# A decoder trunk on one core: on which tiles of an expert block the pieces of gather and scatter are given, and behind which block gathering begins

## The chip, the core and the metric

One core of one Trainium2 chip runs the whole program. The metric is the device time of one execution in microseconds (us), lower is better. TensorE (PE; its weight loads are shown as PEld), VectorE (DVE), ScalarE (ACT), GpSimd (POOL) and SyncE (SP, which issues the loads of weights here) run their own instruction streams and wait for each other through semaphores.

## What is computed

Two layers of a decoder trunk for 256 tokens of width 1024, all in float32. Each layer has four token mixers, an output projection, a feed-forward part and a gated embedding. The feed-forward part of the second layer, the only place that the change touches, sends each token to the best two of eight experts:

```python
def swiglu(x, w_gate, w_up, w_down):
    return (jax.nn.silu(x @ w_gate) * (x @ w_up)) @ w_down

def moe_swiglu(x, router, w_gate, w_up, w_down):
    logits = (x @ router).astype(jnp.float32)
    top_val, top_idx = lax.top_k(logits, TOP_K)
    top_w = jax.nn.softmax(top_val, axis=-1)
    combine = jnp.sum(jax.nn.one_hot(top_idx, N_EXPERTS, ...) * top_w[..., None], axis=-2)
    out = jnp.zeros_like(x)
    for e in range(N_EXPERTS):
        out = out + combine[..., e:e + 1] * swiglu(x, w_gate[e], w_up[e], w_down[e])
    return out
```

An expert's hidden width is 3584.

## The kernel before, in words

**Places.** The eight experts are worked off in eight places, four large ones, L 0 to L 3 (up to 128 tokens, as the stationary side of 128 columns), and four small ones, S 0 to S 3 (up to 64 tokens; high and low halves of the tokens lie side by side in 128 columns). L 0 is the first expert; which experts go to the other places is found at run time by their numbers of tokens. A large and a small place run together, the small one a block behind.

**Blocks and tiles.** Each place has seven blocks of 512 hidden columns (NB = 7), and each block six weight tiles of 1 MB (128 x 2048 floats): t = 0 and 1 are gate tiles, 2 and 3 up tiles, 4 and 5 down tiles. The list STEPS fixes the order of all tiles. In the middle of the stage a block has twelve: L t0, S t0, L t1, then the two turns, S t1, L t2, S t2, L t3, S t3, and then the down tiles of the block before: L t4, S t4, L t5, S t5. An L tile is 12 matmuls of 512 columns (L283 to L285), an S tile 8 (L1344, L1345).

**A weight tile's way.** SP loads it into one of seven buffers `raw` (L212). Products are made of split numbers: ACT copies `raw` to `hi`, DVE subtracts to get `lo` (both in `split`; ACT and DVE instructions of the stage all show as L146, the wrapper that keeps each of the two engines in program order). There are five buffers `hi` and `lo`; `ahead(5, 1)` ahead of each tile keeps the splits of the coming tiles issued, so they stand in the queues of ACT and DVE ahead of whatever follows the tile. PE is kept in program order too (`in_order`).

**Turns.** Between L t1 and S t1 the hidden values of the block before are turned (`turn`): for L four transposes into a PSUM tile `e` (L300) and a split by ACT and DVE; for S sixteen matmuls of 64 columns into another tile `e` (L288), a SiLU on ACT, and then two closures: `times` (a DVE product that reads the same tile `e`) and `parts` (a split into `hs`). There are two PSUM banks for tiles `e`.

**Pieces.** `gather` fetches the tokens of the next two places: six DVE instructions make 0/1 selectors in `s` from `posx`, and then the list `later` gets a pause, four pieces (each 8 matmuls of 192 columns into a tile `e`, L288, then a split of the L columns into `x` by ACT and DVE and one of the S columns into `xs` by ACT and DVE) and two `turned_slots` (two transposes into a tile `e`, L300, an ACT copy). `scatter` splits a finished place's sums at once and puts two pauses and four pieces in `later`: each 2 matmuls of 512 columns into a tile `e` (L288) and one DVE instruction that adds to `h`. The main loop calls `some(1)` after every tile, which takes one entry off `later`. `turn` puts `times` and `parts` at its front, so that they come behind S t1 and L t2. Gathering for the places n + 1 begins behind the second down tile of block 4 of place L n.

So before the change, pieces come behind L t0, S t0, L t1, (turns, `times`, `parts`,) S t2, L t3 and so on, until the list is empty. An L place's scatter is called behind L t5 of the block after its last one, an S place's a block later behind S t5.

Of the kernel before, what the change touches and what calls it, by code (L numbers as in the profile page):

```python
# [84 lines left out]
def decoder_trunk(ctx: ExitStack, tc: tile.TileContext, A, out):  # L85
# [27 lines left out]
    def T(tag, shape, dt=F32, keep=False):  # L113
        count[0] += 1
        name = f"{tag}_{count[0]}"
        if phase and tag + "+" in phase["bufs"] and not keep:
            n = BUFS[tag] + phase["bufs"][tag + "+"]
            turn[tag] = (turn.get(tag, -1) + 1) % n
            if turn[tag] >= BUFS[tag]:
                return phase["pool"].tile(shape, dt, name=name, tag=tag + "+", bufs=n - BUFS[tag])  # L120
        if tag in BUFS and (keep or not (phase and tag in phase["bufs"])):
            return sb.tile(shape, dt, name=name, tag=tag, bufs=BUFS[tag])
        return phase["pool"].tile(shape, dt, name=name, tag=tag, bufs=phase["bufs"][tag])

    def PS(tag, shape, dt=F32):
        count[0] += 1
        return ps.tile(shape, dt, name=f"p{tag}_{count[0]}", tag="p" + tag, bufs=BUFS[tag])
# [96 lines left out]
    def split(x, o_hi, o_lo, note=True):  # L224
        a = act_copy(o_hi, x)
        b = V.tensor_tensor(o_lo, x, f(o_hi), op=ALU.subtract)  # L226
        if note:
            latest.update(act=a, dve=b)
        return a, b
# [4 lines left out]
    def ahead(n, parts=2, keep=False):  # L234

        while len(ready) < n:
            ready.append(new_split(parts, keep))
# [15 lines left out]
    @contextmanager  # L253
    def in_order():

        line.append(None)
        yield
        line.clear()
# [28 lines left out]
    def mm(o, l, r, start=True, stop=True):  # L287
        pe(PE.matmul(o, l, r, start=start, stop=stop, skip_group_check=True))  # L288
# [10 lines left out]
    def transpose(o, i):  # L299
        pe(PE.transpose(o, i, ident[:i.shape[0], :i.shape[0]]))  # L300
# [715 lines left out]
    def feed_forward(i, g_ffn, acc, rest):  # L1016
# [38 lines left out]
        if i == 0:  # L1055
            acc = ffn(xh, xl)
        else:
            acc = None
            moe(cn, xh, xl)
            embed = embedding()  # L1060
            for t in range(2):
                embed(t)
# [104 lines left out]
    def moe(cn, xh, xl):  # L1167
# [153 lines left out]
                if (kind, n) != ("L", 0):  # L1321
                    later.append(partial(turned_slots, kind, n, s, at_[kind]))

        later = []

        def pause():
            pass
# [19 lines left out]
        def gate_up(u, t):  # L1347

            gx = xg[u[:2]]
            g, q = divmod(t, 2)  # L1350
            if q == 0:
                out_[u] = PS("c", [P, 512])
            o = out_[u]
            wh, wl = [v.rearrange("p (k n) -> p k n", k=4) for v in pop_split(1)]
            for kk in range(4):
                k = 4 * q + kk
                lhs = (gx[:, 0, k, :], gx[:, 1, k, :]) if u[0] == "L" else gx[:, k, :]
                products(u, o, lhs, wh[:, kk, :], wl[:, kk, :], k == 0, k == NK - 1)
            if q == 0:
                return  # L1360
            if u[0] == "S":
                s = T("S2", [P, 512])
                act_copy(s, o)
                hid.setdefault(u, []).append(s)
            elif g == 0:
                s = T("S2", [P, 512])
                S.activation(s, o, AF.Silu)
                hid[u] = s
            else:
                V.tensor_tensor(hid[u], hid[u], o, op=ALU.mult)  # L1370

        def turn(u):

            s = hid.pop(u)
            if u[0] == "L":
                pt = PS("e", [P, 4, P])
                for c in range(4):
                    transpose(pt[:, c, :], s[:, c * P:(c + 1) * P])
                hh, hl = T("S2", [P, 4, P], F32R), T("S2", [P, 4, P], F32R)
                split(pt, hh, hl)  # L1380
                hT[u] = hh, hl
                return
            pt = PS("e", [P, 2, 4, 64])
            for g in range(2):
                for c in range(4):
                    mm(pt[:, g, c, :], s[g][:, c * P:(c + 1) * P], cf[:, CF["halves"]])
            a = T("S1", [P, 4, 64])
            S.activation(a, pt[:, 0], AF.Silu)

            def times():  # L1390
                V.tensor_tensor(a, a, pt[:, 1], op=ALU.mult)

            def parts():
                hs = T("S2", [P, 4, P], F32R)
                split(a, hs[:, :, :64], hs[:, :, 64:])
                hT[u] = hs

            later[:0] = [times, parts]

        def down(u, q):  # L1400
            p, b = u[:2], u[2]
            if b == 0 and q == 0:
                acc[p] = [PS("d" if u[0] == "L" else "c", [P, 512]) for _ in range(2)]
            wh, wl = [v.rearrange("p (k n) -> p k n", k=2) for v in pop_split(1)]
            for n in range(2):
                for kk in range(2):
                    c = 2 * q + kk
                    lhs = [v[:, c, :] for v in hT[u]] if u[0] == "L" else hT[u][:, c, :]
                    products(u, acc[p][n], lhs, wh[:, kk, n * 512:(n + 1) * 512],
                             wl[:, kk, n * 512:(n + 1) * 512], b == 0 and c == 0, b == NB - 1 and c == 3)  # L1410
            if q:
                del hT[u]
                if b == NB - 1:
                    scatter(p)
# [18 lines left out]
        def some(n=None):  # L1433
            while later and n != 0:
                later.pop(0)()
                n = n and n - 1
# [15 lines left out]
        with in_order():  # L1452
            for u, t in STEPS:
                if t is None:
                    for v in u:
                        turn(v)
                    done = dict(latest)
                    continue
                ahead(5, 1)
                if t < 4:  # L1460
                    gate_up(u, t)
                else:
                    down(u, t - 4)
                some(1)
                if t == 5 and u[0] == "L" and u[2] == 4 and u[1] < 3:
                    gather(("L", u[1] + 1), ("S", u[1] + 1))
        V.keep(False)
        S.keep(False)
# [227 lines left out]
```

## Time and profile before

| | |
|---|---|
| Time, median of 3 runs | 1669.14 us (1667.97 to 1673.68) |
| Profiled execution | 1667.4 us, of which the span 1665.4 us |
| PE, DVE, ACT busy, share of the span | 95%, 78%, 65% |
| Mean granted clock of PE | 0.973 |
| Expert stage, from its first to its last products | 690 to 1607 us of the span |
| Weights loaded in it | 336 tiles of 1 MB |

Times in rows are counted from the span's start. [...] "Idle before" is the time for which an engine sat idle ahead of an instruction, and behind the arrow stands what ended it. An instruction is shown in a group by the tiles it writes and reads (`pe`, `pc`, `pd` are PSUM tiles of the tags e, c, d).

### The profile page before, as it was taken

To read this page: it belongs to the slowest core of one execution; us is meant where nothing else is said; L and a number is where in the kernel's file an instruction comes from. 1 tells how busy PE (TensorE), PEld (TensorE's weight loads), DVE (VectorE), ACT (ScalarE), POOL (GpSimd) and SP (SyncE) were. 2 spreads that over 40 slices of the span, in tenths; PEclk is the share of its full clock that TensorE was granted. 3 is DMA by queue.
4 is the path that set the end of the run, shared out by engine and by line. 5 is a ranking of instruction groups with operands and counts; after the bars stand their busy time and mean duration, and the time that the engine had idled before them with its cause. 6 is when DMAs were issued, how large, how long until landed. Compare 5 with 4: busy or idle time off the path is not lost.

```text
span 1665.4 us, 22588 instructions
## 1 busy us (share of the span) xinstructions
PE 1580.6 (95%) x8523; PEld 1347.7 (81%) x8523; DVE 1299.9 (78%) x1464; ACT 1085.9 (65%) x1309; POOL 80.4 (5%) x116
## 2 busy tenths in 40 slices
PE   7998999999999989799989999989999989999998
PEld 7896799999888977688878778878778877788886
DVE  5578655445575786799979889979889979799995
ACT  5555554444455563688868668858768867688883
POOL 1024000000000141000000000000000000000000
PEclk9999999999999999899999999999999999899999
DMA  8431464545444222499999889979989979899980
GB/s 323 161 118 58 159 233 159 213 160 204 144 163 184 98 98 77 166 421 421 421 378 377 347 332 413 415 310 388 350 338 416 419 284 416 343 349 415 420 361 26
DMA packets 65488, 461.25 MB, mean 277 GB/s; under 512 B 7392, under 2 KB 7776, under 8 KB 12128
## 3 DMA queue, kind: packets, MB, share of 16 engines
q1 hardware_dynamic: 64224, 455.02, 69.4%
q10 hardware_dynamic: 1152, 4.76, 0.9%
q8 instruction: 68, 1.11, 0.3%
q14 instruction: 44, 0.36, 0.1%
HBM read 458.70 MB, written 1.05 MB: 276 GB/s over the span
## 4 chain that ended last, share of the span: by engine, by line
PE 38%; DVE 11%; issue 6%; ACT 2%; DMA 1%; POOLq 0%; POOL 0%; DVEq 0%; ACTq 0%
DVE lo L146 8%; PE pc L1344 7%; PE pc L1345 6%; PE pc L283 5%; PE pc L285 4%; PE pc L284 4%; PE pe L288 4%; ACT hi L146 2%; PE pd L283 2%; PE pd L284 2%; PE pd L285 2%; DMA raw<-in_moe_gu_dram 1%; DVE S L146 1%; DVE h L146 1%; PE pe L300 1%
## 5 line engine op out<-in xcount | busy, mean ns | idle before, releaser
L146 DVE TENSOR_TENSOR lo<-raw,hi 128x2048 fp32r<-128x2048 f32 x338 | 757.9, 2284 | 94.6 <-ACT hi L146 94.2
L146 ACT ACTIVATE hi<-raw 128x2048 fp32r<-128x2048 f32 x338 | 637.2, 1911 | 79.1 <-PE pd L285 23.1
L226 DVE TENSOR_TENSOR lo<-raw,hi 128x1024 fp32r<-128x1024 f32 (+3 forms) x188 | 201.2, 1113 | 122.7 <-ACT hi L160 122.4
L160 ACT ACTIVATE hi<-raw 128x1024 fp32r<-128x1024 f32 (+3 forms) x188 | 170.0, 966 | 120.4 <-PE pc L285 84.3
L283 PE MATMUL pc<-hi,x 128*128 128x512 f32 x512 | 203.6, 398 | 3.1 <-DVE order L1263 2.4
L285 PE MATMUL pc<-hi,x 128*128 128x512 f32 x512 | 202.0, 394 | 0.0
L284 PE MATMUL pc<-lo,x 128*128 128x512 f32 x512 | 202.0, 394 | 0.0
L1344 PE MATMUL pc<-hi,xs 128*128 128x512 f32 x448 | 186.5, 416 | 0.0
L283 PE MATMUL pd<-x,hi 128*128 128x256 f32 x640 | 182.4, 285 | 0.1
L1345 PE MATMUL pc<-lo,xs 128*128 128x512 f32 x448 | 182.4, 407 | 0.0
L285 PE MATMUL pd<-x,lo 128*128 128x256 f32 x640 | 182.1, 285 | 0.0
L284 PE MATMUL pd<-x,hi 128*128 128x256 f32 x640 | 181.5, 284 | 0.3 <-DVE x L226 0.3
L283 PEld LDWEIGHTS pd<-x,hi 128*128 128x128 f32 x640 | 122.4, 191 | 1.6 <-ACT x L160 0.3
L285 PEld LDWEIGHTS pd<-x,lo 128*128 128x128 f32 x640 | 122.3, 191 | 1.5 <-DVE lo L226 0.2
L284 PEld LDWEIGHTS pd<-x,hi 128*128 128x128 f32 x640 | 122.3, 191 | 1.2 <-DVE x L226 0.5
L283 PEld LDWEIGHTS pc<-hi,x 128*128 128x128 f32 x512 | 96.9, 189 | 25.5 <-issue 2.6
L285 PEld LDWEIGHTS pc<-hi,x 128*128 128x128 f32 x512 | 96.5, 188 | 22.8 <-DVE x L226 0.4
L284 PEld LDWEIGHTS pc<-lo,x 128*128 128x128 f32 x512 | 96.5, 188 | 22.1
L1344 PEld LDWEIGHTS pc<-hi,xs 128*128 128x128 f32 x448 | 88.9, 198 | 19.1
L1345 PEld LDWEIGHTS pc<-lo,xs 128*128 128x128 f32 x448 | 88.6, 198 | 19.3
L288 PE MATMUL pe<-cf,S 128*128 128x64 f32 (+1 forms) x452 | 66.4, 310 | 26.1 <-DVE h L146 13.2
L283 PE MATMUL pd<-hi,S 128*128 128x512 f32 x224 | 88.7, 396 | 0.0
(288 smaller groups left out, 2510.0 us busy)
## 6 DMA issues: line engine op xcount, KB each, us to landing
raw<-in_moe_gu_dram SPq DMA_DIRECT2D x224, 1024.0 KB, 7.1
raw<-in_moe_dn_dram SPq DMA_DIRECT2D x112, 1024.0 KB, 7.8
raw<-in_ffn_gu_dram SPq DMA_DIRECT2D x28, 1024.0 KB, 5.1
raw<-in_ffn_dn_dram SPq DMA_DIRECT2D x14, 1024.0 KB, 5.0
raw<-in_win_t_dram SPq DMA_DIRECT2D x16, 848.0 KB, 4.7
raw<-in_win_c_dram SPq DMA_DIRECT2D x12, 1024.0 KB, 6.6
raw<-in_cmp_w_dram SPq DMA_DIRECT2D x8, 1024.0 KB, 5.6
raw<-in_w_out_dram SPq DMA_DIRECT2D x8, 1024.0 KB, 4.9
```

Source lines behind the costliest of these rows:

```text
L146: ins = op(*args, **kw)
L160: return S.activation(o, i, AF.Copy, scale=scale)
L226: b = V.tensor_tensor(o_lo, x, f(o_hi), op=ALU.subtract)
L283: pe(PE.matmul(o, lh, rh, start=start, stop=False))
L284: pe(PE.matmul(o, lh, rl, start=False, stop=False))
L285: pe(PE.matmul(o, ll, rh, start=False, stop=stop))
L288: pe(PE.matmul(o, l, r, start=start, stop=stop, skip_group_check=True))
L300: pe(PE.transpose(o, i, ident[:i.shape[0], :i.shape[0]]))
L1344: pe(PE.matmul(o, lhs, rh, start=start, stop=False))
L1345: pe(PE.matmul(o, lhs, rl, start=False, stop=stop))
```

## The change

There are now two lists. `times` and `parts` go to a list `soon`. Behind each tile the loop takes an entry of `soon` if there is one; if there is none, it takes one of `later`, but only behind tiles with t of 2 to 5 (and behind every tile of the very first block). And `gather` is called behind block 3 of a place L n instead of block 4.

```diff
-        later = []
+
+        soon, later = [], []
...
-            later[:0] = [times, parts]
+            soon.extend([times, parts])
...
-                some(1)
-                if t == 5 and u[0] == "L" and u[2] == 4 and u[1] < 3:
+                if soon:
+                    soon.pop(0)()
+                elif t > 1 or u == ("L", 0, 0):
+                    some(1)
+                if t == 5 and u[0] == "L" and u[2] == 3 and u[1] < 3:
                     gather(("L", u[1] + 1), ("S", u[1] + 1))
```

## Rows read from the trace of the kernel before

**Rows 1.** The page's first part, the line of PE: busy us (share of the span), instructions.
```profile
PE 1580.6 (95%) x8523; PEld 1347.7 (81%) x8523; DVE 1299.9 (78%) x1464; ACT 1085.9 (65%) x1309; POOL 80.4 (5%) x116
```

**Rows 2.** Busy time by stretches, each from the start of one S turn to that of the next. Columns: stretch, its length, busy us and instructions of PE, PEld, DVE, ACT, POOL, then granted clock, busy share of the DMA engines, GB/s.
```profile
764.39:794.37 29.98, 29.98 (x143) 24.71 (x142) 28.82 (x17) 25.35 (x18) 0.00 (x0) 1.00 1.01 421
...
824.28:864.61 40.33, 34.35 (x167) 28.51 (x165) 35.72 (x30) 29.63 (x27) 0.00 (x0) 0.98 1.01 421
864.61:899.13 34.52, 34.52 (x152) 28.83 (x153) 27.03 (x18) 25.24 (x22) 0.00 (x0) 0.92 0.83 315
899.13:934.30 35.17, 31.80 (x148) 25.68 (x146) 33.86 (x24) 27.04 (x22) 0.00 (x0) 1.00 1.01 423
934.30:972.12 37.82, 35.08 (x147) 28.43 (x147) 31.74 (x22) 26.09 (x20) 0.00 (x0) 0.91 0.86 327
972.12:1006.33 34.21, 34.21 (x145) 28.26 (x146) 28.07 (x18) 24.36 (x17) 0.00 (x0) 0.90 0.85 318
1006.33:1036.36 30.03, 30.03 (x143) 24.70 (x141) 28.21 (x17) 25.00 (x19) 0.00 (x0) 1.00 1.01 420
```

**Rows 3.** Groups of instructions by line and shape in the stretch 690 to 1610 us, the two groups of PE matmuls with idle time ahead of them (the S turns; the L turns with the slots' transposes). Behind the first bar busy us and mean ns of one, behind the second the idle us before them and what ended it.
```profile
L288 PE MATMUL pe<-cf,S 128*128 128x64 f32 x448 | 65.8, 310 | 25.7 <-DVE h L146 13.2 <-DVE xs L146 12.4
...
L300 PE MATMUL pe<-cf,S 128*128 128x128 f32 x126 | 19.8, 275 | 9.3 <-DVE h L146 5.9 <-DVE xs L146 3.4
```

**Rows 4.** Stretches of the expert stage in which the granted clock is 0.50 (columns as in Rows 2): the first of nine, the sum over the three that lie behind gather pieces, and the sum over all nine.
```profile
863.31:870.14 6.83, 5.53 (x21) 5.18 (x22) 1.50 (x4) 2.61 (x4) 0.00 (x0) 0.50 0.95 396
...
sum 20.49, PE 18.46 PEld 16.80 DVE 4.43 ACT 7.73 POOL 0.00; mean PE 6.15 PEld 5.60 DVE 1.48 ACT 2.58 POOL 0.00
...
sum 54.63, PE 50.63 PEld 45.27 DVE 12.03 ACT 21.56 POOL 0.00; mean PE 5.63 PEld 5.03 DVE 1.34 ACT 2.40 POOL 0.00
```

**Rows 5.** The two whole rounds of seven blocks, from the S turn behind one gather to that behind the next (columns as in Rows 2).
```profile
864.61:1105.58 240.97, 229.97 (x1032) 189.16 (x1033) 210.68 (x138) 180.09 (x141) 0.00 (x0) 0.96 0.93 372
1105.58:1345.32 239.74, 228.21 (x1032) 187.97 (x1033) 210.53 (x138) 180.08 (x141) 0.00 (x0) 0.96 0.92 368
```

**Rows 6.** Timeline of PE (above) and DVE (below) around the first gather of two places: start us, length us, engine, line, operation, tiles, shapes, count, and in brackets the idle time before it and what ended it. On PE the four pieces, the product behind the first one, and the first slot's transposes; on DVE the last operation on each piece and the weight splits behind the first two.
```profile
849.32 1.46 PE L288 MATMUL pe<-S,C 128*128 128x192 f32 x8
850.48 0.52 PE L1344 MATMUL pc<-hi,xs 128*128 128x512 f32 x1
...
852.47 1.46 PE L288 MATMUL pe<-S,C 128*128 128x192 f32 x8
...
856.53 1.46 PE L288 MATMUL pe<-S,C 128*128 128x192 f32 x8
...
875.58 1.46 PE L288 MATMUL pe<-S,C 128*128 128x192 f32 x8
879.68 0.38 PE L300 MATMUL pe<-cf,S 128*128 128x128 f32 x2
...
854.62 0.29 DVE L146 TENSOR_TENSOR xs<-pe,xs 128x128 fp32r<-128x128 f32 x1 [0.34 <-ACT xs L146]
856.43 2.29 DVE L146 TENSOR_TENSOR lo<-raw,hi 128x2048 fp32r<-128x2048 f32 x1 [1.52 <-ACT hi L146]
...
859.40 0.29 DVE L146 TENSOR_TENSOR xs<-pe,xs 128x128 fp32r<-128x128 f32 x1 [0.34 <-ACT xs L146]
861.20 2.29 DVE L146 TENSOR_TENSOR lo<-raw,hi 128x2048 fp32r<-128x2048 f32 x1 [1.51 <-ACT hi L146]
...
864.17 0.29 DVE L146 TENSOR_TENSOR xs<-pe,xs 128x128 fp32r<-128x128 f32 x1 [0.34 <-ACT xs L146]
...
879.07 0.29 DVE L146 TENSOR_TENSOR xs<-pe,xs 128x128 fp32r<-128x128 f32 x1 [0.34 <-ACT xs L146]
```

**Rows 7.** The same two views around the first scatter of a large place: on PE the first two pieces and the product behind the first one, on DVE the two additions to `h` that read them.
```profile
924.10 0.62 PE L288 MATMUL pe<-S,S 128*128 128x512 f32 x2
924.56 0.40 PE L1344 MATMUL pc<-hi,xs 128*128 128x512 f32 x1
...
926.40 0.63 PE L288 MATMUL pe<-S,S 128*128 128x512 f32 x2
...
927.79 0.74 DVE L146 SCALAR_TENSOR_TENSOR h<-pe,comb,h 128x512 f32<-128x512 f32 x1
...
930.65 0.74 DVE L146 SCALAR_TENSOR_TENSOR h<-pe,comb,h 128x512 f32<-128x512 f32 x1
```

**Rows 8.** The dense feed-forward stage of the first layer, by comparison: a stretch of it (columns as in Rows 2), and from the timeline of PE the first and the last of twelve 512-column matmuls in a row.
```profile
300.00:350.00 50.00, 50.00 (x356) 46.93 (x354) 25.52 (x30) 21.87 (x30) 0.00 (x0) 1.00 0.50 182
...
333.41 0.39 PE L283 MATMUL pc<-hi,S 128*128 128x512 f32 x1
...
335.98 0.40 PE L285 MATMUL pc<-hi,S 128*128 128x512 f32 x1
```

**Rows 9.** Timeline of DVE in a block without pieces: the split behind the L turn, `times` behind the S turn, and the gate product behind L t3.
```profile
768.75 0.68 DVE L146 TENSOR_TENSOR S<-pe,S 128x512 fp32r<-128x512 f32 x1
...
771.81 0.41 DVE L146 TENSOR_TENSOR S<-S,pe 128x256 f32<-128x256 f32 x1
...
779.08 0.68 DVE L146 TENSOR_TENSOR S<-S,pc 128x512 f32<-128x512 f32 x1
```

**Rows 10.** Who waited for whom in the stretch 690 to 1610 us, the row of ACT's `xs` operations: us in total, times, longest.
```profile
ACT xs L146 <- DVE x L146: 24.1, 12, 2.9
```

**Rows 11.** The instructions that read `posx` in that stretch, the selectors of three gathers: shortest, median and longest in ns, first and last start, shapes.
```profile
L146 DVE TENSOR_SCALAR S<-cf,posx x18: 245/255/285, 848.4 to 1330.0; 128x64 f32<-128x64 f32 x12, 128x128 f32<-128x128 f32 x6
```

## Prediction

> **What bounds the kernel now.** The page comes first [rows 1]: PE is busy 95% of the span, yet "busy" hides two things, so I cut the expert stage (690 to 1607 us, more than half the span) into its blocks, from one S turn to the next [rows 2]. An undisturbed block takes 30.0 us. In it PE never pauses, the granted clock is 1.00, and the loads run at 421 GB/s with the DMA engines 1.01 busy: PE and the loads both just fit, DVE is at 28.8 and ACT at 25.4. The blocks in which rows are gathered for the next places (ends 864.61) or scattered back (ends 934.30 and 972.12) take 35 to 40 us, and those after them 34.2 to 34.5 at a mean clock of 0.90 to 0.92. Nothing is caught up later: the next clean block is 30.03 again. So the losses add to the span.
>
> What is lost is in the waits of PE [rows 3]: in the whole stage the view names no others of it than those for DVE, 13.2 + 5.9 = 19.1 us for `h` (scatter pieces) and 12.4 + 3.4 = 15.8 us for `xs` (gather pieces), all at the matmuls of the two turns: 34.9 us. [...] Sum 60.2 us: gather 15.8 + 9.2 (its three stretches hold 18.5 us of PE) = 25.0; scatter 19.1 + 16.1 = 35.2.
>
> A second way to the same sum starts from whole rounds of seven blocks, 240.97 and 239.74 us [rows 5]. Seven clean blocks are 7 x 30.0 = 210. A gather piece is 1.16 us of PE (849.32 to 850.48), a slot transpose 0.14, a scatter piece 0.46 (924.10 to 924.56) [rows 6, 7]: 4 x 1.16 + 2 x 0.14 + 8 x 0.46 = 8.6. Floor 218.6, excess 22.4 and 21.1 a round, about 65 for three. The ways differ by 5 us, which I keep as uncertainty.
>
> **Why the turns wait.** Tiles `e` have two PSUM banks. Before the change the pieces follow the two gate tiles (L t0, S t0) and L t1, and the turns come immediately behind: the L turn needs the bank of the second piece, the S turn that of the third. A bank is free when its last reader is done, and the readers stand in DVE's queue behind weight splits of 2.2 us. The three gather pieces ended on PE 1.16 after their starts, at 850.48, 853.63 and 857.69, and DVE's last `xs` operation on them (start plus length) at 854.91, 859.69 and 864.46: 4.4, 6.1 and 6.8 us, growing because a piece holds DVE up by 4.76 us (split start 856.43 to next split start 861.20) while PE spends 2.3 to 2.8 + 1.16 [rows 6]. The fourth, alone at an up tile, took 2.6 us and nobody waited. For the first two scatter pieces of a place it is 4.0 us (924.56 to 928.53) and 4.5 (926.86 to 931.39) [rows 7].
>
> **The change, part by part.** It adds and removes no instruction. In every block after the first it keeps the queued pieces from L t0, S t0 and L t1; S t1 and L t2 still take `times` and `parts`, as before; pieces then go at S t2, L t3, S t3 and the four down tiles. No DMA is moved and SP's queue isn't touched.
>
> Scatter pieces. For a finished L place they move from L t0, S t0, L t1, S t2 to S t2, L t3, S t3, L t4; for S one tile later. Two pieces of the same bank then lie one L tile, one S tile and one piece apart. A 512-column matmul starts every 0.233 us (333.41 to 335.98 is 11 of them) [rows 8], so the distance is 20 x 0.233 + 0.46 = 5.1 us, above the 4.0 to 4.5 that freeing takes. The turns' own banks are free in time: in a clean block whose S turn starts at 764.39, DVE reads the L turn until 769.43 and the S turn until 772.22 [rows 9]; S t2 ends some 1.7 + 28 x 0.233 = 8.2 us after that start, at 772.6, and its piece needs only the first of the two. At the next turn both banks have long been free. So I price scatter's remaining waits at 0, the whole 35.2 us gone. If the cover (5.1 against 4.5) is used up by the 0.68 us of the gate product that DVE has at L t3 (779.08) [rows 9], 0.1 us comes back at two pieces of each of six scatters: 1.2 us.
>
> Gather pieces. Now four come on consecutive tiles: S t2, L t3, S t3, L t4, then the two slot transposes at S t4 and L t5. Same-bank distance is 20 x 0.233 + 1.16 = 5.8 us. Piece 3 needs piece 1 (4.4): no wait. Piece 4 needs piece 2 (6.1): 0.3. The L slots need piece 3 (6.8), 5.8 + 0.3 later: 0.7. The S slots need piece 4: by the growth of 0.7 a piece some 7.3 us, and 8 x 0.233 + 0.14 + 0.7 + 12 x 0.233 = 5.5 have gone: 1.8. About 2.5 us after I allow that freeing starts lower (DVE comes in with six tiles between its selectors and the first piece, where before they were adjacent). Bounds: 0 (each freed as fast as piece 4 of today) and 5.3 (15.8 / 3, all of today's wait at the slots). I take 2.5, since the latencies come from the same pieces. Three gathers: 7.5 us left, 15.8 - 7.5 and the clock's 9.2 saved.
>
> The four readers of a gather piece are serial: ACT's `xs` operation waited for DVE's `x` 12 times, 24.1 us in all [rows 10], though both only read. [...]
>
> One block earlier. The gather call, with six DVE selectors of some 0.255 us [rows 11], moves from behind block 4 to behind block 3. The buffers it writes were last read at least four blocks before, and its pieces take 15 us of the 60 before the new place starts; with the call left where it is they would fit as well, in the next block. So by itself this costs and gives 0; the selectors cost 1.5 us of DVE either way, covered by DVE's 1.2 us of room a block and the tiles split ahead. If that cover were gone it would be 3 x 1.5 = 4.6 us. Turns, `times` and `parts` keep their places: 0.
>
> **Sum.** By the first way 60.2 - 7.5 = 52.7 us, by the second 65 - 7.5 = 57.5; I take 55. From the profiled execution's 1667.4 us (span 1665.4 and 2.0 around it) that gives 1612.4; the median lies 1.7 above this execution, so **1614**. The clock may still fall behind the S slots' 1.8 us. Today it fell at all nine turns, where the waits are 3.9 us on average (34.9 / 9) [rows 3, 4]; I take it that it stays up at 1.8, and three stretches of 6.83 would cost 10 us.
>
> **Rivals.**
> - A. The gather stall keeps its size and only moves from the turns to the slots, clock included (the growth of 0.7 a piece speaks for it, the 5.8 us distance against). Only scatter's 35.2 goes: 1634.
> - B. Scatter waits stay (DVE, with the gate product at L t3, frees banks over 5.1 us late) and only gather's go: 25.0 - 7.5 = 17.5, so 1652.
> - C. The change doesn't do what it says: as many waits at the pieces themselves as there were at the turns. 1669. Against it: today's fourth pieces, on up tiles, were waited for by nobody.
> - D. Slower. The waits don't vanish but are spread over the tiles of the pieces, 10 to 14 us long, so that the clock is down for one more stretch of 6.83 at each of nine places: 9 x 3.41 = 31 us, 1700. It decides when freeing a bank takes some 2 us more than its distance, over 7 us for scatter pieces; the longest read is 4.5.
> - E. PE has slack in a clean block and only the loads bind. Then a round is 7 x 29.9 = 209 (pieces hidden), 31 less than today, 93 for three: 1576. Against it stand the 0.233 us, which hold too where the DMA share is 0.50 [rows 8], and that today's clean blocks catch nothing up. [...]
>
> **How the numbers follow.** Forecast 0.70 (1604, all of the 65 gone, to 1624, the clock falling at each gather), A 0.13, B 0.05, C 0.05, D 0.05, E 0.02. Range 1604 to 1636: forecast and A, 0.83. Faster by over 0.3% (about what a measurement of this kernel can tell from no change): 0.70 + 0.13 + 0.05 + 0.02 = 0.90; same 0.05, slower 0.05.
>
> **What would show it.** Waits of PE for `h` in the stage: none over 0.5 us. Waits for `xs`: at the transposes of the slots, not at the turns, at most 3 us a gather. Gather blocks 37.4 us (30.0 + 4.9 + 2.5), scatter blocks 31.9 (30.0 + 4 x 0.46), all others 30.0 at clock 1.00. Wrong would make it: stretches at 0.50 behind the pieces, PE waiting for `lo` (splits late), or DMA waits in clean blocks.

## The result, and the profile after

| | before | changed |
|---|---|---|
| Time, median | 1668.56 us (4 runs) | 1614.43 us (1611.28 to 1616.45, 4 runs) |
| Ratio to before | | 0.9669, 95% interval 0.9642 to 0.9696 |
| Profiled execution, span | 1667.4, 1665.4 us | 1613.72, 1611.9 us |

The forecast was 1614. The span is split at two marks: the first S turn of the stage that has a block of twelve tiles ahead of it (734.36 and 734.59 us) and the last S turn (1607.11 and 1551.38). First the kernel before, then the changed one; columns are stretch, length, busy us and instructions of PE, PEld, DVE, ACT, POOL, granted clock, DMA share, GB/s.

```profile
734.36:1607.11 872.75, 837.81 (x3815) 690.21 (x3814) 779.19 (x497) 671.09 (x515) 0.00 (x0) 0.97 0.94 380
1607.11:1665.42 58.31, 50.86 (x225) 39.97 (x223) 39.74 (x46) 28.93 (x40) 1.08 (x2) 0.97 0.24 96
```
```profile
734.59:1551.38 816.79, 810.90 (x3814) 669.38 (x3813) 777.41 (x497) 668.54 (x516) 0.00 (x0) 1.00 0.99 406
1551.38:1611.94 60.56, 52.55 (x225) 41.08 (x223) 39.74 (x46) 28.91 (x40) 1.08 (x2) 0.94 0.23 93
```

Two rows of a kernel are enough to see where the time went. In the stage length less PE's busy time is PE's waiting: 34.94 us before, 5.89 after. The busy time itself falls from 837.81 to 810.90 for the same matmuls, 26.91 us. Most of that is the clock, 0.97 before and 1.00 after. An S turn in a clean block of the kernel before, and one in the first of its nine stretches at 0.50 [rows 4], with the matmuls behind it:

```profile
764.39 1.90 PE L288 MATMUL pe<-cf,S 128*128 128x64 f32 x16
766.09 0.48 PE L1344 MATMUL pc<-hi,xs 128*128 128x512 f32 x1
...
864.61 3.65 PE L288 MATMUL pe<-cf,S 128*128 128x64 f32 x16 [4.15 <-DVE xs L146]
868.01 0.77 PE L1344 MATMUL pc<-hi,xs 128*128 128x512 f32 x1
868.59 0.63 PE L1345 MATMUL pc<-lo,xs 128*128 128x512 f32 x1
...
869.87 0.53 PE L1344 MATMUL pc<-hi,xs 128*128 128x512 f32 x1
```

From start to start the turn takes 3.40 us at 0.50, where it takes 1.70 at 1.00. Matmuls of 512 columns start every 0.427 us there (868.59 to 869.87 is three of them), where they take 0.233 [rows 8]. Of the 50.6 us for which PE is busy in the nine stretches, 23.6 belong to turns and 27.1 to such matmuls. By an estimate from these figures the clock cost 11.8 + 12.3 = 24.1 us. The other 2.8 seem to go with the waits themselves, for a kernel without any wait, the last but one below, is busy for 810.01 us, another 0.9 less at the same clock. 29.05 + 26.91 = 55.96 us, the whole shortening of the stage. Behind the stage 2.3 us are given back, and 0.2 ahead of it.

All waits of PE in the stage that the changed kernel has left (us in total, times, longest), where the kernel before had four such entries, 34.9 us together [rows 3]:

```profile
PE pe L300 <- DVE xs L146: 5.9, 4, 1.8
```

Blocks from one S turn to the next, as in [rows 2], and one whole round, as in [rows 5]:

```profile
764.61:794.58 29.97, 29.97 (x142) 24.70 (x141) 28.84 (x17) 25.36 (x18) 0.00 (x0) 1.00 1.01 421
824.49:863.28 38.79, 36.04 (x178) 30.12 (x177) 31.02 (x25) 28.07 (x29) 0.00 (x0) 1.00 0.95 386
863.28:893.40 30.12, 30.12 (x143) 24.71 (x142) 30.12 (x18) 25.88 (x20) 0.00 (x0) 1.00 1.00 408
...
923.41:955.21 31.80, 31.80 (x151) 26.22 (x149) 31.36 (x23) 26.11 (x21) 0.00 (x0) 1.00 1.01 416
955.21:987.13 31.92, 31.92 (x150) 26.20 (x149) 31.92 (x21) 25.21 (x19) 0.00 (x0) 1.00 1.01 403
987.13:1017.17 30.04, 30.04 (x143) 24.71 (x141) 29.45 (x18) 25.00 (x19) 0.00 (x0) 1.00 1.01 414
1047.16:1084.71 37.55, 35.95 (x179) 30.10 (x177) 29.55 (x24) 26.24 (x28) 0.00 (x0) 1.00 0.84 323
```
```profile
863.28:1084.71 221.43, 219.84 (x1035) 181.34 (x1033) 210.10 (x139) 179.42 (x141) 0.00 (x0) 1.00 0.98 398
```

A block with scatter takes 31.8 to 31.9 us with PE busy all of it: its four pieces cost just their own PE time (4 x 0.46 = 1.84 us). The block behind a disturbed one takes 30.0 to 30.1, where it took 34. Only the gather blocks hold waits. Their timeline shows where: on PE the four pieces and the two slot transposes of the second gather, on DVE the last operation on each piece.

```profile
1055.46 1.46 PE L288 MATMUL pe<-S,C 128*128 128x192 f32 x8
...
1059.52 1.46 PE L288 MATMUL pe<-S,C 128*128 128x192 f32 x8
...
1062.68 1.46 PE L288 MATMUL pe<-S,C 128*128 128x192 f32 x8
...
1066.79 1.46 PE L288 MATMUL pe<-S,C 128*128 128x192 f32 x8
...
1069.93 0.41 PE L300 MATMUL pe<-cf,S 128*128 128x128 f32 x2
...
1074.72 0.41 PE L300 MATMUL pe<-cf,S 128*128 128x128 f32 x2 [1.59 <-DVE xs L146]
```
```profile
1059.36 0.29 DVE L146 TENSOR_TENSOR xs<-pe,xs 128x128 fp32r<-128x128 f32 x1 [0.34 <-ACT xs L146]
...
1064.72 0.29 DVE L146 TENSOR_TENSOR xs<-pe,xs 128x128 fp32r<-128x128 f32 x1 [0.34 <-ACT xs L146]
...
1069.50 0.29 DVE L146 TENSOR_TENSOR xs<-pe,xs 128x128 fp32r<-128x128 f32 x1 [0.34 <-ACT xs L146]
...
1074.28 0.29 DVE L146 TENSOR_TENSOR xs<-pe,xs 128x128 fp32r<-128x128 f32 x1 [0.34 <-ACT xs L146]
```

With 1.16 us of PE a piece, freeing (from the piece's end to the end of DVE's last read) takes 3.0, 4.3, 6.0 and 6.6 us: growing from piece to piece as in [rows 6], but begun lower. The fourth piece's bank is free at 1074.57; the S slots, which PE has come to at 1073.1, need it. The third gather is like this one (3.1, 4.4, 6.0, 6.7). In the first, freeing takes 4.2, 5.5, 7.1 and 8.0 us, and there the L slots wait too (0.99 us, then the S slots 1.76).

Around the first scatter of a large place, PE's first two pieces and DVE's two additions that read them: freeing takes 3.5 us (932.09 to 935.60) and 3.7 (935.34 to 939.06), and no one waits.

```profile
931.63 0.62 PE L288 MATMUL pe<-S,S 128*128 128x512 f32 x2
...
934.88 0.63 PE L288 MATMUL pe<-S,S 128*128 128x512 f32 x2
```
```profile
934.85 0.75 DVE L146 SCALAR_TENSOR_TENSOR h<-pe,comb,h 128x512 f32<-128x512 f32 x1
...
938.31 0.75 DVE L146 SCALAR_TENSOR_TENSOR h<-pe,comb,h 128x512 f32<-128x512 f32 x1
```

### The profile page after: what moved, and what is told of

It is laid out like the page before. It is cut to its first block, busy times and chain, and to the rows that moved or that the text cites. A ratio compares the mean times of both kernels' runs of the same rounds, so it can differ in the third digit from the quotient of the medians.

```text
span 1611.9 us, 22583 instructions
## 1 busy us (share of the span) xinstructions
PE 1555.2 (96%) x8523; PEld 1327.7 (82%) x8523; DVE 1297.9 (81%) x1464; ACT 1083.1 (67%) x1309; POOL 80.5 (5%) x116
## 3 DMA queue, kind: packets, MB, share of 16 engines
q10 hardware_dynamic: 1152, 4.76, 0.9%
## 4 chain that ended last, share of the span: by engine, by line
PE 43%; DMA 4%; DVE 4%; ACT 3%; issue 3%; SPq 0%; POOLq 0%; POOL 0%; ACTq 0%
PE pc L1345 8%; PE pc L1346 8%; PE pc L285 5%; PE pc L283 5%; PE pc L284 5%; PE pe L288 3%; DMA raw<-in_moe_gu_dram 3%; DVE lo L146 3%; PE pd L283 3%; PE pd L284 3%; PE pd L285 3%; ACT hi L146 2%; DMA raw<-in_moe_dn_dram 1%; PE pe L300 1%; DVE S L146 0%
## 5 line engine op out<-in xcount | busy, mean ns | idle before, releaser
L1345 PE MATMUL pc<-hi,xs 128*128 128x512 f32 x448 | 178.9, 399 | 0.0
L1346 PE MATMUL pc<-lo,xs 128*128 128x512 f32 x448 | 176.3, 393 | 0.0
L1346 PEld LDWEIGHTS pc<-lo,xs 128*128 128x128 f32 x448 | 84.2, 188 | 18.2
L1345 PEld LDWEIGHTS pc<-hi,xs 128*128 128x128 f32 x448 | 84.2, 188 | 18.0
L1345 PE MATMUL pc<-hi,S 128*128 128x512 f32 x224 | 88.8, 396 | 0.0
```

What stands on the lines that cost most here:

```text
L1345: pe(PE.matmul(o, lhs, rh, start=start, stop=False))
L1346: pe(PE.matmul(o, lhs, rl, start=False, stop=stop))
```

## The experiments

The theory on trial (bank theory): the turns waited for PSUM banks that pieces behind the tiles just ahead of them held until DVE had read them, and the clock fell behind those waits. Rivals: the earlier start brings the gain; any piece ahead of the turns costs, wherever it stands (number theory). The kernel before took 1668.2 beside the first four runs and 1667.8 beside the others. A kernel with a third tile `e`, the plainest test of the banks, was not run.

### The two halves of the change

Gathering a block earlier alone (the kernel before with this edit):

```diff
-                if t == 5 and u[0] == "L" and u[2] == 4 and u[1] < 3:
+                if t == 5 and u[0] == "L" and u[2] == 3 and u[1] < 3:
```

> Only the second half of the change: gathering begins behind block 3, pieces go on every tile as before. Bank theory (the turns wait for PSUM banks that pieces on the tiles ahead of them hold): the same pieces stand ahead of the same turns, one block earlier, so nothing changes: 1669, within 5 us. Rival (the earlier start brings the gain, since the new place finds its tokens ready): most of the 54 us, 1615 to 1630.

Measured 1671.2, ratio 1.0016 (1.0005 to 1.0027), 3 us slower and within the 5 allowed. Its waits are those of before, to 0.2 us a row:

```profile
PE pe L288 <- DVE h L146: 13.2, 6, 2.2
PE pe L288 <- DVE xs L146: 12.4, 3, 4.1
PE pe L300 <- DVE h L146: 6.1, 6, 1.3
PE pe L300 <- DVE xs L146: 3.6, 3, 1.8
```

The 3 us lie in PE's busy time between the marks, 840.7 us where it was 837.8: the nine stretches at 0.50 add up to 64.9 us there, and to 54.6 in the kernel before [rows 4]; over the whole span the granted clock is 0.970 and 0.973. Why they are longer isn't shown.

Holding the pieces back alone (the changed kernel with block 4 again):

```diff
-                if t == 5 and u[0] == "L" and u[2] == 3 and u[1] < 3:
+                if t == 5 and u[0] == "L" and u[2] == 4 and u[1] < 3:
```

> Only the first half of the change: pieces held back from gate tiles, gathering still begins behind block 4. Bank theory: the whole gain, 1614, within 4 us; the pieces of a gather still end a block ahead of the place that needs them. Rival (the earlier start is needed): waits for the gathered tokens at the new place's first tiles, 1630 or more.

Measured 1609.72, ratio 0.9653 (0.9631 to 0.9676), 0.3 us beyond the 4 allowed. So the whole gain is in the holding back, and the earlier start brings nothing; the 4.7 us by which this run lies below the changed kernel are looked into below.

### The two kinds of pieces

A list `free` holds the pieces of one kind, which go behind every tile as before; the other kind is held back. For the run with scatter held (the gather call at block 4; for the run with gather held, `scatter` fills `free` in the same way and the call stays at block 3):

```diff
-                elif t > 1 or u == ("L", 0, 0):
+                elif t > 1 or u == ("L", 0, 0) or (later and later[0] in free):
                     some(1)
...
+            free.extend(mine)
+            later.extend(mine)
```

> Scatter's pieces are held back from gate tiles, gather's go on every tile and begin behind block 4 as before. Bank theory, by the prediction's split: 35 of the 60 us go, 1633 to 1636; waits for h gone, waits for xs at the turns 15 to 16 us as before, clock at 0.50 behind three turns. Rival (DVE is simply short of time and any relief is shared): waits for xs fall as well.

> Gather's pieces are held back and begin behind block 3, scatter's go on every tile as before. Bank theory: 25 less the 6 us left at the slots go, 1648 to 1652; waits for h 19 us as before. With the run in which only scatter is held the two gains add up to that of the whole change, 54; a gain that is smaller alone than in the sum would speak for a shared cause.

Scatter held: 1630.97, ratio 0.9779 (0.9755 to 0.9803), 37.2 us. Gather held: 1650.57, ratio 0.9893 (0.9871 to 0.9915), 17.6 us. Together 54.8, beside the changed kernel's 54.1. In the first, three stretches at 0.50 are left in the stage, as expected (6.8, 6.8 and 10.2 us), and waits for `h` are gone and those for `xs` are the old ones to a tenth; in the second it is the other way round, with the 5.8 us at the slots that the changed kernel has as well:

```profile
PE pe L288 <- DVE xs L146: 12.4, 3, 4.1
PE pe L300 <- DVE xs L146: 3.4, 3, 1.8
```
```profile
PE pe L288 <- DVE h L146: 13.2, 6, 2.2
PE pe L300 <- DVE h L146: 5.8, 6, 1.3
PE pe L300 <- DVE xs L146: 5.8, 4, 1.8
```

### Is it the bank or the number of pieces?

One queued piece may go ahead of the turns again, either behind L t0 or behind L t1 (the changed kernel, with one of these):

```diff
-                elif t > 1 or u == ("L", 0, 0):
+                elif t > 1 or u == ("L", 0, 0) or (u[0], t) == ("L", 0):
...
+                elif t > 1 or u == ("L", 0, 0) or (u[0], t) == ("L", 1):
```

> The changed kernel, but one queued piece may go behind L t0 as well, two tiles ahead of the turns. Bank theory: a piece there leaves one of the two banks free for the L turn, and the S turn needs its bank 1.9 + 2.8 + 0.4 = 5.1 us later, when it is free (4.0 to 4.5); so no wait at the turns and the time of the changed kernel, within 5 us: 1610 to 1619. Rival (number theory: each piece ahead of the turns costs, since DVE reaches the turns' work later; today three stand there): a third of the gain is lost, 1632.

> The changed kernel, but one queued piece may go behind L t1, immediately ahead of the turns. That concerns the first piece of each of three gathers and of three L scatters; the S scatters have a pause there. Bank theory: the L turn takes the other bank, the S turn needs that of the piece 0.4 us behind it, and waits the freeing time less that, about 4 us, at six S turns, with the clock down behind each: 6 x (3.8 + 2 to 3.4) = 35 to 43 more than the changed kernel, 1650 to 1657. Number theory: the same as behind L t0, 1632.

Behind L t0: 1612.63 (1611.77 to 1613.45), the changed kernel's time. Its first gather shows the piece on PE, DVE's last read of it and the S turn, which needs the same bank:

```profile
819.63 1.54 PE L288 MATMUL pe<-S,C 128*128 128x192 f32 x8 [0.19 <-DVE S L146]
...
826.08 1.90 PE L288 MATMUL pe<-cf,S 128*128 128x64 f32 x16
```
```profile
825.04 0.29 DVE L146 TENSOR_TENSOR xs<-pe,xs 128x128 fp32r<-128x128 f32 x1 [0.34 <-ACT xs L146]
```

The bank is free at 825.33, 0.75 us before the turn, and the turn doesn't wait.

Behind L t1: 1643.66, 29 us more than the changed kernel's 1614.43. One and the same piece costs nothing two tiles ahead of the turns and 5 us directly ahead of them, so number theory falls. In the second run PE waits at the S turns again (first two rows; the third is what is left at the slots):

```profile
PE pe L288 <- DVE h L146: 9.7, 3, 3.3
PE pe L288 <- DVE xs L146: 9.2, 3, 3.8
PE pe L300 <- DVE xs L146: 1.4, 3, 0.5
```

and the timeline of its first gather shows the two users of `e` on PE behind the piece, the L turn at once, the S turn only when DVE's last read of the piece is done (829.33 + 0.29, 4.4 us after the piece's end):

```profile
824.03 1.46 PE L288 MATMUL pe<-S,C 128*128 128x192 f32 x8
825.33 0.60 PE L300 MATMUL pe<-cf,S 128*128 128x128 f32 x4
829.77 3.65 PE L288 MATMUL pe<-cf,S 128*128 128x64 f32 x16 [3.84 <-DVE xs L146]
```
```profile
829.33 0.29 DVE L146 TENSOR_TENSOR xs<-pe,xs 128x128 fp32r<-128x128 f32 x1 [0.34 <-ACT xs L146]
```

I had put 1650 to 1657: six waits of 3.8 us. They were 18.9 us in all, 3.2 each, and the piece's absence from the later tiles took 4.5 us off the waits at the slots. PE's busy time in the stage is 18.4 us longer than in the changed kernel, within what I had put for the clock; behind the stage 2.6 us are won.

### What sets the freeing time

If banks are the cause, freeing them sooner must help where nothing else is changed. The kernel before, with ACT's reads of a gather piece ahead of DVE's:

```diff
                 for kind, n in places:
                     w = P if kind == "L" else 64
-                    split(o[:, :, at_[kind]:at_[kind] + w], *[v[:, k * q:k * q + k] for v in dst[kind]])
+                    cut.append((o[:, :, at_[kind]:at_[kind] + w], *[v[:, k * q:k * q + k] for v in dst[kind]]))
+                for src, hi, lo in cut:
+                    latest["act"] = act_copy(hi, src)
+                for src, hi, lo in cut:
+                    latest["dve"] = V.tensor_tensor(lo, src, f(hi), op=ALU.subtract)
```

> The kernel before, with one edit: ACT takes its two reads of a gather piece (x, xs) one behind the other and DVE then its two, so that the four readers change engine once and not three times. Bank theory, with the freeing time as the thing that counts: ACT no longer waits for DVE between x and xs (24 us in all), DVE loses less (4.76 us a piece falls to some 3.5), so freeing grows less from piece to piece and the waits for xs at the turns fall from 15.8 to 5 to 10 us; 5 to 15 us faster with the clock, 1654 to 1664. Rival (the freeing time is set by the splits in DVE's queue alone, the order of the readers is hidden): no change, 1668.

Measured 1648.19, ratio 0.9883 (0.9863 to 0.9903): 20 us, more than I had expected. The waits for `xs` fall from 15.8 to 3.6, and with them the clock's three stretches behind gather pieces go: the six that are left in the stage lie at the scatters.

```profile
PE pe L288 <- DVE xs L146: 3.6, 3, 1.7
```

On DVE a piece now takes 2.73 us from the start of one split to the start of the next (854.20 to 856.93), where it took 4.76 [rows 6]; both figures include the split itself, 2.2 us:

```profile
854.20 2.28 DVE L146 TENSOR_TENSOR lo<-raw,hi 128x2048 fp32r<-128x2048 f32 x1
856.40 0.41 DVE L146 TENSOR_TENSOR x<-pe,x 128x256 fp32r<-128x256 f32 x1
856.74 0.28 DVE L146 TENSOR_TENSOR xs<-pe,xs 128x128 fp32r<-128x128 f32 x1
856.93 2.28 DVE L146 TENSOR_TENSOR lo<-raw,hi 128x2048 fp32r<-128x2048 f32 x1
```

In the old order ACT, between its two reads, waited for DVE's turn (24.1 us in 12 waits), and behind them DVE for ACT's next split (1.5 us behind each of the first two pieces) [rows 6, 10]. Only the number of hand-overs between the two has changed. In the first gather they still don't read the first piece's bank at once: ACT's two reads end at 851.38, and DVE's two begin at 853.67, behind two weight splits. Whether they could, no run shows.

Two pauses ahead of the slots' transposes, in the changed kernel:

```diff
+            if len(places) == 2:
+                later.extend([pause, pause])
             for kind, n in places:
                 if (kind, n) != ("L", 0):
                     later.append(partial(turned_slots, kind, n, s, at_[kind]))
```

> The changed kernel, with two pauses between the fourth gather piece and the transposes of the slots, so that these come two tiles later. Bank theory: the 5.9 us of waits at the slots go, and what the clock may lose behind them in some executions: 1606 to 1609. Rival (the waits move to the next user of a bank, the L turn of the next block): no change, 1614.

Measured 1608.57, ratio 0.9645 (0.9628 to 0.9661). The waits at the slots are gone, but in the profiled execution half of them come back as something new, PE waiting for weights:

```profile
PE pc L1348 <- DVE lo L146: 2.7, 3, 1.7
```

I read this as the splits being behind after four pieces of 4.76 us on consecutive tiles, which the wait at the slots had hidden; that was not tried apart. The last run below, which has the other order of readers as well and gathers behind block 4, shows no such wait.

### The last four, in the same rounds

These four were measured together, on one chip.

> The changed kernel unaltered, on the same chip and in the same rounds as the next run, to settle the 4.7 us by which the kernel with only the holding back was faster. Its profile beside that of the changed kernel: 0.7 us in the expert stage, the rest ahead of the stage and behind it, where one more stretch of 3.4 and one of 6.8 us runs at clock 0.50. Theory (the earlier start costs at most 1 us; the rest is where the clock's fall happens to lie from chip to chip): the two agree within 2 us. Rival (beginning a block earlier costs 3 to 5 us): 1614 against 1610 again.

> Only the first half of the change, as in the second run. Theory: within 2 us of the changed kernel in these rounds. Rival: 3 to 5 us faster than it.

The changed kernel again 1612.92, holding back alone 1609.67: 3.2 us apart, more than I had allowed. The profiles put 0.3 of it in the stage (816.47 and 816.15 us between the marks) and 0.2 ahead of it. The rest is behind the last S turn, from here on the tail, in identical work, first the changed kernel, then the other:

```profile
1550.56:1611.13 60.57, 52.55 (x225) 41.09 (x223) 39.74 (x46) 28.93 (x40) 1.09 (x2) 0.94 0.23 93
```
```profile
1550.07:1607.89 57.82, 49.81 (x225) 38.94 (x223) 39.65 (x46) 28.93 (x40) 1.09 (x2) 0.99 0.25 97
```

PE's busy time differs by 2.74 us at clock 0.94 and 0.99. So the earlier start costs under 1 us itself, and neither theory had it: the tail ran at a mean clock of 0.94 in both profiles of the changed kernel, and at 0.99 in both of the other. The run that comes next begins gathering early too and has a tail of 57.8 us, so the early start alone doesn't decide it; what does isn't settled.

> The changed kernel with the other order of the readers of a gather piece (ACT's two, then DVE's two). In the kernel before this order took 20 us. Bank theory: in the changed kernel only the 5.9 us at the slots are left to it, so 4 to 7 us: 1607 to 1611, no wait for xs above 0.5 us. Rival (the order saves DVE time that counts by itself, whatever the banks do): 10 us or more, 1604 or less.

> All that helped in one: pieces held back, gathering behind block 4 as before, readers in the other order, two pauses ahead of the slots. Theory: no wait of PE for a bank is left in the expert stage, clock 1.00 throughout it, blocks with a gather at 30.0 + 4.9 = 34.9, with a scatter at 31.9; 6 us below the run with only the holding back: 1603 to 1607. Rival (the loads bind as soon as PE waits for nothing): no lower than the third run of this set, with PE waiting for lo.

The other order of readers in the changed kernel gives **1603.69** (1602.37 to 1606.59), ratio 0.9621 (0.9607 to 0.9634), the best of all; everything together 1606.34, ratio 0.9631 (0.9618 to 0.9644). By its time alone the first would meet the rival's figure (9.2 us under the changed kernel of these rounds), but in the profiled executions, which lie 10.5 us apart, 6.5 are between the marks, as the theory had it, and no wait for `xs` is left; 2.8 are the tail, 57.8 against 60.6, and 1.3 lie ahead of the stage.

The last run lies in its range, 1603 to 1607, but only 3.3 us below holding back alone, where I had put 6, and by its time alone its rival (no lower than the third) would hold too. PE waits for no `lo`, though, and between the marks it is 5.8 us shorter than holding back alone. Between the marks the third and the fourth are equal, 810.01 and 810.34 us; what sets them apart lies outside the stage. The row of the best one:

```profile
732.78:1542.79 810.01, 810.01 (x3815) 669.85 (x3813) 777.04 (x498) 670.20 (x516) 0.00 (x0) 1.00 1.00 409
```

PE is busy for every one of the 810.01 us, at a granted clock of 1.00. There is no wait left between the marks to remove.

## Why the prediction was right

The mechanism was right: the pieces held the banks that the turns needed, and held back they hold nobody up but the slots. That the time came within 0.5 us of 1614 is in part luck, as the terms show.

**The waits at the turns and the clock** were the whole of it, as the first way of the sum had them: waits 34.9, and 26.9 of busy time, where I had 9.2 + 16.1 = 25.3 from the nine half-clock stretches. That 25.3 is half of PE's 50.6 us in them, which no run shows: the S turns took half as long at 1.00 (1.70 us for 3.40), matmuls of 512 columns 0.55 of their time (0.233 for 0.427), and the nine come to about 24.1. What was left came out at 5.9, I had 7.5. With these figures in its terms the first way gives 34.9 + 26.9 - 5.9 = 55.9, and the stage became 56.0 shorter. My 55 was a middle of 52.7 and 57.5. The second way was the nearer for the stage, and for whole rounds it was met: a floor of 218.6 and the 2.5 left make 221.1, measured 221.43 and 221.10. The first was the nearer for the whole program, which became 54.1 shorter.

**Scatter at 0**: held, freeing takes 3.5 and 3.7 us, less than before, against a distance of 5.1. Alone it gave 37.2, forecast 35.2.

**Gather at 2.5 a place**: 2.75 in the first gather, 1.6 in the two others. In the first the terms came as written: 0.99 at the L slots (I had 0.7) and 1.76 at the S slots (1.8), with freeing times of 7.1 and 8.0 us. In the two others freeing began lower (3.0 us), the third piece came free after 6.0 us and not 6.8, and the L slots didn't wait. The 0.3 at piece 4 came in none. Alone it gave 17.6, forecast 25.0 - 7.5 = 17.5. One reading was off without weight: between the first three pieces PE spent 2.0 and 2.9 us on the tiles, not 2.3 to 2.8 [rows 6].

**The earlier start at 0**: in the stage 0.3 to 0.7 us. What I had not seen is the tail, which was 2.7 us longer in the changed kernel than with holding back alone: my sum had no term for the clock outside the stage. The 2.3 us given back there, and 0.2 ahead of the stage, are why 56.0 became 53.5 in the profiled execution, and why 1614 was met so closely: two small errors of opposite sign, which is luck.

**The rivals.** A (the gather stall moves whole) would have shown 15.8 us of waits for `xs`; 5.9 remained. B would have left 19 us of waits for `h`; none is left. C falls with both. D needed the clock to fall at the pieces; it stayed at 1.00 throughout the stage. E (PE has slack) is refuted by the scatter blocks: they grew by 1.8 to 1.9 us, the PE time of four pieces, so the loads alone don't bind. PE was busy for all of each, though in the second, 31.92 us, DVE was too. Matmuls of 512 columns start every 0.233 us here [rows 8]; by an estimate the 120 of a clean block fill 28.0 of its 30.0 us, and the two turns, 2.1 us in the kernel before (763.95 to 766.09), the rest.

## What to carry to other kernels

Where two PSUM banks serve several kinds of small work, count for each use how long its bank takes to come free (its last reader's place in the queue, not the reader's own length: 4.4 to 6.8 us for the three gather pieces ahead of the turns before the change, with last reads of 0.29 us), and compare it with the PE time until the next use of the same bank: one piece two tiles ahead of the next user cost nothing, directly ahead of it 5 us. Here nine pairs of waits of PE, 2.7 to 6.0 us a pair, cost by the estimate above some 0.7 times as much again through the clock (24.1 beside 34.9), so length less busy time and the busy time itself are to be read together. And before work is moved away from a bottleneck, look at the order of its readers: changing that order alone took 20 us off the kernel before, with no piece moved.

## What was unexpected in the hardware

The clock behind the last expert block: the same instructions with nearly the same waits of PE (1.69 and 0.67 us in the changed kernel, 1.69 and 0.66 with holding back alone) ran in 57.8 us where the granted clock stayed up behind them (0.99 over the tail), and in 60.6 where a stretch of 6.83 us at 0.50 followed (from 1580.53 us in the changed kernel). The kernel before, with a stretch of 3.41 us, lies between (58.3). The two kernels that were profiled twice had the same tail both times (60.56 and 60.57; 57.82 and 57.82), which speaks against chance from run to run; what it depends on, these runs don't show.
